# Attention of a hybrid encoder: scores as three products of high and low parts, made in the second projection stage

## Chip, cores and metric

The kernel runs on one core of a Trainium2 chip, as one program with one launch. The metric is device microseconds (us) of one execution. Engines are named as in the profile: PE is TensorE (matmuls), PEld its weight loads, DVE is VectorE, ACT is ScalarE, POOL is GpSimd, SP is SyncE, which here issues most DMAs. An L with a number is a line of the kernel before.

## What is computed

A two-layer encoder over 2048 prompt tokens and 32 sampled tokens, model width 1024. Layer 0 is a gated DeltaNet. From its output h come shared keys and values, and layer 1 is a sliding-window attention over them. The part that the change touches, cut from the reference:

```python
k, v = shared_kv(h, w_kv, pos)               # 4 key heads of 64, partial rotary on k
proj = h @ w_in
q = rope_partial(proj[..., :1024].reshape(b, l, 16, 64), pos) * 64 ** -0.5
z = proj[..., 1024:]
# queries of chunk n (64 tokens) see the keys of chunks n-2, n-1, n
s = jnp.einsum('bnqkgd,bnskd->bnkgqs', qb, kb, preferred_element_type=jnp.float32)
p = sink_softmax(s, sinks)                    # one learned sink logit per head
o = jnp.einsum('bnkgqs,bnskd->bnqkgd', p, vb)
out = (o * jax.nn.silu(z)) @ w_out            # then residual and layer norm
```

## The kernel before

All large products are written as three products of float32r tiles: an operand x is kept as hi = float32r(x) and lo = float32r(x - hi), and hi*hi + hi*lo + lo*hi is accumulated (`project`, L79 to L81). Small products, the scores among them, use plain float32 operands, for which the program has two MATMUL instructions per product.

The work goes through stages: the first projection, the delta rule with layer 0's output beside it, the second projection (its value products start at 1324 us of the span, its last matmul before the hand-written order ends at 1719 us) and attention (first score at 1728.3 us).

**Second projection (class `P2`).** The tokens lie in five blocks of TB = 416 columns. `rotated` makes two key slabs and eight query slabs of 128 rows (i = 0 to 9), each for five blocks b: 24 matmuls into one PSUM bank, of which there are eight here; then `rope` (ACT copies the bank to tile ra at L1343, DVE shuffles it at L1344, POOL multiplies by the sine at L1345, DVE multiplies and adds at L1346 and L1347), and one DMA on SP stores ra to the DRAM scratch bk or bq (L1409, L1412). Tiles ra and rs come from pool `wk` with three buffers, so the bank of block k can be copied only when the store of block k-3 has landed. Beside it, `keep_out_weights` splits the output weights (tiles wo_parts) on ACT and POOL and stores them to the scratch wob. `gate` makes the gate slabs: ACT writes zs and za (L1428, L1429) into the same two tags of pool `wk`, DVE multiplies, and SP stores za to the scratch bz (L1431). The order in this stage comes from the scheduler of the framework.

**Attention (class `Attention`).** The order is written out by hand for all five engines (`manual_schedule`), each of which runs its instructions in that order. Chunks are taken as 14 to 31, then 0 to 13. Before: the keys are loaded in three stretches into one tile kT that stays (`load_keys`, L1491: chunks 12 to 17 first, 18 to 31 next, 0 to 11 last); `start(n)` loads the queries of chunks n and n+1, two DMAs of 256 KB (L1676); `gate(n)` loads their gates (L1681). `scores(n, p)` makes for each of two p four products of 64 rows by 128 by up to 192 columns (L1698), the two halves of which lie on rows 0 to 63 and 64 to 127 of the array. Then softmax (DVE L1518, ACT L1523, POOL L1537), transposes (L1713), copies to tile pt (ACT L1719, DVE L1720), products with the values (`values`, L1731) and, once for two chunks, the output projection (L1146 to L1148) and the layer norm.

At the start of attention eight last blocks of gate slabs 4 to 7 are still to be made; the function `gates` in `program` makes them piece by piece between the first chunks, and among them issues the loads of two weight slabs (L48), of keys and values for the later chunks and of the first output weights (`load_early`, L1468: EARLY = 3 of 8 pieces, 1024 KB each). When the pools of the second projection are closed, `opened` loads the remaining pieces (`load_late`, L1484), and the last keys. The output projection of the first two chunks needs all eight pieces.

Of the kernel before, what the change touches and what calls it, by code (L numbers as in the profile page):

```python
# [22 lines left out]
NP = 2048  # L23
NS = 32
# [1267 lines left out]
class P2:  # L1292
# [100 lines left out]
    def rotated(self):  # L1393
# [6 lines left out]
        for i in range(10):  # L1400
            w = split_weights(nc, self.wp, I["w_k"][i] if i < 2 else I["b_w_in"][i - 2], nc.gpsimd)
            for b in range(NB):
# [4 lines left out]
                if i >= 2:  # L1407
                    a = self.rope(ps[:, :TB], b, 0.125)
                    nc.sync.dma_start(T["bq"][i - 2, :, b * TB:(b + 1) * TB], a[:])  # L1409
                    continue  # L1410
                a = self.rope(ps[:, :TB], b, 1.0)
                nc.sync.dma_start(T["bk"][i, :, b * TB:(b + 1) * TB], a[:])  # L1412
                if b == NB - 1:
                    nc.scalar.dma_start(O["k_last"][i, :, :], a[:, TB - 160:TB])
                    nc.scalar.dma_start(O["s_kT"][i, :, 96:128], a[:, TB - NS:TB])
# [18 lines left out]
class Attention:  # L1434


    EARLY = 3

    def __init__(self, tc, left, I, O, T, G):
# [10 lines left out]
        self.kT = one.tile([128, 2, NP], F32, tag="kT", name="kT")  # L1450

# [37 lines left out]

    def load_keys(self, a, z):  # L1490
        self.nc.sync.dma_start(self.kT[:, :, a * 64:z * 64],  # L1491
                               self.T["bk"][:, :, a * 64:z * 64].rearrange("a p t -> p a t"))
# [119 lines left out]
    def sampled_keys(self):  # L1612
        nc, I, T, one, two = self.nc, self.I, self.T, self.one, self.two
        ks = one.tile([128, 2, 160], F32, tag="ks", name="ks")
        nc.sync.dma_start(ks[:, :, 0:128], I["cache_kT"].rearrange("a p t -> p a t"))
        nc.sync.dma_start(ks[:, :, 128:160], T["bk"][:, :, NP:NT].rearrange("a p t -> p a t"))
        vc = one.tile([128, 256], F32, tag="vc", name="vc")
        nc.sync.dma_start(vc[:], I["cache_v"])
        vn = one.tile([32, 256], F32, tag="vn", name="vn")
        nc.sync.dma_start(vn[:], T["bv"][NP:NT, :])  # L1620
        qs = two.tile([128, 8, NS], F32, tag="qs", name="qs")
        zs = two.tile([128, 8, 128], F32, tag="zs", name="zs")
        nc.sync.dma_start(qs[:], T["bq"][:, :, NP:NT].rearrange("h p t -> p h t"))
# [47 lines left out]
    def start(self, n):  # L1671

        qs = self.two.tile([128, 2, 8, 64], F32, tag="qs", name="qs")
        for i in range(2):
            tk = (n + i) * 64
            self.nc.sync.dma_start(qs[:, i], self.T["bq"][:, :, tk:tk + 64].rearrange("h p t -> p h t"))  # L1676
        self.data[n], self.data[n + 1] = [qs, None], [qs, None]
# [10 lines left out]
    def scores(self, n, p):  # L1688

        nc = self.nc  # L1690
        qs = self.data[n][0]
        kc0, nj = self.keys(n)
        nk = nj * 64
# [537 lines left out]
```

## Time and profile before

| what | value |
|---|---|
| median of 3 runs | 2122.08 us (2119.59 to 2124.72) |
| the profiled execution | 2119.22 us, of which its span 2117.1 us |
| granted TensorE clock in it | 0.996 |
| PE busy | 2078.8 us, 98% of the span |
| POOL, ACT, DVE busy | 39%, 43%, 62% |
| DMA | 307.26 MB, 145 GB/s on the mean |

The profile is one execution. A busy PE is one on which some matmul is under way, since matmuls are pipelined: two rows that start 0.19 us apart may each last 0.35 us. The time between two starts is therefore the pace, the length of a row is not. The view by stretches gives the busy time of each engine between two times, the granted clock, the mean busy share of the 16 DMA engines, and GB/s. The chain of work that ended last follows each instruction back to what released it.

### The profile page before, as it was taken

What the parts mean: (1) busy time and instruction counts of PE and PEld (TensorE: products, weight loads), DVE (VectorE), ACT (ScalarE), POOL (GpSimd) and SP (SyncE); (2) the same over time, 40 slices, a digit from 0 to 9 for tenths busy, and PEclk for the clock granted to TensorE, in tenths of its full rate; (3) what the DMA queues carried; (4) which work ended last, traced back from release to release, by engine and by line L of the source; (5) the groups of instructions that cost most, each with busy time, mean ns of one, the idle gap of its engine ahead of it and who ended that gap; (6) DMA issues with size and microseconds to landing.
All of it is one profiled execution on the core that took longest, in us unless ns stands there. A gap on an engine that the chain in (4) does not pass through costs nothing.

```text
span 2117.1 us, 37205 instructions
## 1 busy us (share of the span) xinstructions
PE 2078.8 (98%) x14062; PEld 1912.6 (90%) x14062; DVE 1306.6 (62%) x2449; ACT 901.1 (43%) x2263; POOL 834.6 (39%) x1179
## 2 busy tenths in 40 slices
PE   8999999999999999999999999999999998999998
PEld 6999999999999999999888888999999996777775
DVE  4676666666557688889978885225543223566665
ACT  4444444445622377677752212322111233455552
POOL 1422222222122187878830302136443103566765
PEclk9999999999999999999999999999999998999999
DMA  5222332346664545556846764455222257534321
GB/s 206 67 65 82 111 111 92 96 128 207 197 197 153 178 157 180 163 171 210 278 159 204 240 194 131 135 196 202 82 72 70 75 143 259 137 100 120 100 72 65
DMA packets 263636, 307.26 MB, mean 145 GB/s; under 512 B 71409, under 2 KB 194609, under 8 KB 263185
## 3 DMA queue, kind: packets, MB, share of 16 engines
q1 hardware_dynamic: 252208, 281.40, 42.7%
q10 hardware_dynamic: 11248, 23.48, 3.4%
q8 instruction: 111, 1.82, 0.4%
q14 instruction: 69, 0.56, 0.1%
HBM read 188.58 MB, written 116.60 MB: 144 GB/s over the span
## 4 chain that ended last, share of the span: by engine, by line
PE 91%; POOL 3%; DMA 2%; DVE 2%; ACT 1%; issue 1%; SPq 1%; ACTq 0%; POOLq 0%; DVEq 0%
PE ps L79 17%; PE ps L81 17%; PE ps L80 17%; PE ot L1146 3%; PE po L1146 3%; PE po L1148 3%; PE po L1147 3%; PE ot L1148 3%; PE ot L1147 3%; PE S L1698 2%; PE ot L1731 2%; PE tr L1713 2%; POOL tm L729 1%; POOL Tt L731 1%; PE g L695 1%; PE gq L831 1%
## 5 line engine op out<-in xcount | busy, mean ns | idle before, releaser
L79 PE MATMUL ps<-act_hi,w_hi 128*128 128x416 f32 x1936 | 683.3, 354 | 1.4 <-ACT act_hi L70 1.4
L81 PE MATMUL ps<-act_hi,w_lo 128*128 128x416 f32 x1936 | 681.3, 352 | 0.9 <-POOL w_lo L56 0.9
L80 PE MATMUL ps<-act_lo,w_hi 128*128 128x416 f32 x1936 | 678.2, 350 | 0.4 <-DVE act_lo L71 0.4
L79 PEld LDWEIGHTS ps<-act_hi,w_hi 128*128 128x128 f32 x1936 | 364.1, 188 | 6.6 <-ACT act_hi L70 2.1
L80 PEld LDWEIGHTS ps<-act_lo,w_hi 128*128 128x128 f32 x1936 | 363.8, 188 | 4.8 <-DVE act_lo L71 0.8
L81 PEld LDWEIGHTS ps<-act_hi,w_lo 128*128 128x128 f32 x1936 | 363.4, 188 | 4.7 <-POOL w_lo L56 1.3
L56 POOL TENSOR_TENSOR w_lo<-w_raw,w_hi 128x1024 fp32r<-128x1024 f32 x44 | 117.1, 2661 | 470.3 <-ACT w_hi L55 443.1
L209 DVE SCALAR_TENSOR_TENSOR y<-R,convw,y 128x2083 f32<-128x2083 f32 x72 | 182.7, 2538 | 62.8 <-ACT y L206 46.9
L1537 POOL TENSOR_TENSOR P<-e,sm 128x384 f32<-128x384 f32 (+2 forms) x128 | 101.2, 812 | 181.7 <-DVE sm L1527 175.7
L729 POOL TENSOR_TENSOR tm<-L,Tt 128x60 f32<-128x60 f32 (+19 forms) x365 | 133.2, 365 | 78.8 <-issue 39.9
L731 POOL TENSOR_TENSOR Tt<-Tt,tm 128x60 f32<-128x60 f32 (+19 forms) x365 | 140.8, 386 | 28.6
L1523 ACT ACTIVATE e<-S,nm 128x193 f32<-128x193 f32 (+2 forms) x260 | 104.8, 416 | 95.9 <-DVE nm L1518 58.2
L1146 PE MATMUL ot<-wo,g_hi 128*128 128x512 f32 x256 | 104.6, 409 | 6.1 <-DMA wo<-s_wob 6.1
L305 ACT COPY R<-ps 128x416 f32<-128x416 f32 (+1 forms) x144 | 60.3, 442 | 108.3 <-PE ps L81 95.7
L1146 PE MATMUL po<-wo_hi,g_hi 128*128 128x512 f32 x256 | 103.3, 404 | 0.2 <-ACT g_hi L1188 0.2
L1345 POOL TENSOR_TENSOR rs<-rs,sin 128x416 f32<-128x416 f32 x50 | 70.7, 1414 | 80.3 <-DVE rs L1344 73.5
L1148 PE MATMUL ot<-wo,g_lo 128*128 128x512 f32 x256 | 101.2, 395 | 0.0
L1147 PE MATMUL ot<-wo,g_hi 128*128 128x512 f32 x256 | 101.1, 395 | 0.0
L1148 PE MATMUL po<-wo_hi,g_lo 128*128 128x512 f32 x256 | 100.2, 392 | 0.5 <-DVE g_lo L1189 0.5
L1430 DVE SCALAR_TENSOR_TENSOR za<-zs,za 128x416 f32<-128x416 f32 x40 | 31.7, 796 | 111.3 <-ACT za L1429 111.1
L1147 PE MATMUL po<-wo_lo,g_hi 128*128 128x512 f32 x256 | 99.9, 390 | 0.0
L55 ACT CAST w_hi<-w_raw 128x1024 fp32r<-128x1024 f32 x46 | 48.3, 1051 | 93.5 <-PE ps L80 74.4
(299 smaller groups left out, 3917.9 us busy)
## 6 DMA issues: line engine op xcount, KB each, us to landing
w_raw<-in_w_in SPq DMA_DIRECT2D x40, 512.0 KB
w_raw<-in_b_w_in SPq DMA_DIRECT2D x18, 512.0 KB
k<-s_k SPq DMA_DIRECT2D x17, 512.0 KB
E<-s_E SPq DMA_DIRECT2D x17, 512.0 KB
s_bz<-za SPq DMA_DIRECT2D x40, 208.0 KB
s_bq<-ra SPq DMA_DIRECT2D x40, 208.0 KB
s_q<-y SPq DMA_DIRECT2D x8, 1024.0 KB
s_wo<-wo_parts SPq DMA_DIRECT2D x16, 512.0 KB
```

Source lines behind the costliest of these rows:

```text
L56: sub.tensor_tensor(out=lo[:], in0=raw[:], in1=hi[:], op=ALU.subtract)
L79: nc.tensor.matmul(ps, hi[:, k, :], xh[:, k, :], start=(k == 0), stop=False)
L80: nc.tensor.matmul(ps, hi[:, k, :], xl[:, k, :], start=False, stop=False)
L81: nc.tensor.matmul(ps, lo[:, k, :], xh[:, k, :], start=False, stop=(k == KC - 1))
L209: nc.vector.scalar_tensor_tensor(out=y[:], in0=R[:, j:j + W], scalar=self.convw[:, i, j:j + 1], in1=y[:], op0=ALU.mult, op1=ALU.add)
L729: P.tensor_tensor(out=tm[:n, i0 - k:, :w], in0=L[:n, i0:, j:j + 1].to_broadcast(sh), in1=Tt[:n, j:j + 1, :w].to_broadcast(sh), op=ALU.mult)
L731: P.tensor_tensor(out=Tt[:n, i0:, :w], in0=Tt[:n, i0:, :w], in1=tm[:n, i0 - k:, :w], op=ALU.subtract)
L1146: nc.tensor.matmul(ps[:n], ghi[:, k, :n], hi, start=a, stop=False)
L1147: nc.tensor.matmul(ps[:n], ghi[:, k, :n], lo, start=False, stop=False)
L1148: nc.tensor.matmul(ps[:n], glo[:, k, :n], hi, start=False, stop=z)
L1523: self.nc.scalar.activation(x.e[:, h, u, :x.n], x.S[:, h, u, :], AF.Exp, bias=x.nm[:, h, u:u + 1], scale=1.0, accum_out=x.sm[:, h, u:u + 1])
L1537: self.nc.gpsimd.tensor_tensor(out=x.P[:, u, :nj * 128].rearrange("r (j h k) -> r j h k", h=2, k=64), in0=x.e[:, :, u, :n].rearrange("r h ...
```

## The change

Queries and keys are split into hi and lo right after the rotary step, and both parts go to new DRAM scratch tensors. Of the old scratch only the 32 sampled columns remain. In attention the keys no longer stay: `start(n)` loads, for two chunks, a stretch of up to 256 keys in both parts (tile kw, two DMAs of 256 KB) and the queries in both parts (four DMAs of 256 KB). A score is hi*hi + lo*hi + hi*lo in float32r, one MATMUL instruction each. EARLY goes from 3 to 2, and the tiles of the sampled step's keys and values take a slot of kw.

```diff
@@ P2.rotated
-                if i >= 2:
-                    a = self.rope(ps[:, :TB], b, 0.125)
-                    nc.sync.dma_start(T["bq"][i - 2, :, b * TB:(b + 1) * TB], a[:])
-                    continue
-                a = self.rope(ps[:, :TB], b, 1.0)
-                nc.sync.dma_start(T["bk"][i, :, b * TB:(b + 1) * TB], a[:])
+                a = self.rope(ps[:, :TB], b, 0.125 if i >= 2 else 1.0)
+                name, j = ("q", i - 2) if i >= 2 else ("k", i)
                 if b == NB - 1:
...
+                self.keep_parts(T["bparts_" + name][:, j, :, b * TB:(b + 1) * TB], a)
+
+    def keep_parts(self, dst, a):
+        nc = self.nc
+        hi = self.wk.tile([128, TB], F32R, tag="rh", name="rh")
+        lo = a[:].bitcast(F32R)
+        nc.scalar.copy(hi[:], a[:])
+        nc.gpsimd.tensor_tensor(out=lo, in0=a[:], in1=hi[:], op=ALU.subtract)
+        nc.sync.dma_start(dst[0], hi[:].bitcast(F32))
+        nc.sync.dma_start(dst[1], a[:])
@@ Attention
-    EARLY = 3
+    EARLY = 2
...
-        self.kT = one.tile([128, 2, NP], F32, tag="kT", name="kT")
...
-    def load_keys(self, a, z):
...
@@ Attention.start
-        qs = self.two.tile([128, 2, 8, 64], F32, tag="qs", name="qs")
+        k0, k1 = max(0, n - 2) * 64, (n + 2) * 64
+        kw = self.two.tile([128, 2, 2, 256], F32R, tag="kw", name="kw")
+        qs = self.two.tile([128, 2, 2, 8, 64], F32R, tag="qs", name="qs")
+        for a in range(2):
+            self.nc.sync.dma_start(kw[:, a, :, :k1 - k0].bitcast(F32),
+                                   self.T["bparts_k"][a, :, :, k0:k1].rearrange("c p t -> p c t"))
...
@@ Attention.scores
         for u in range(2):
-            for half in range(2):
-                hs = slice(half * 64, half * 64 + 64)
-                nc.tensor.matmul(S[:, half, u, :nk], qs[hs, n % 2, p * 4 + 2 * u:p * 4 + 2 * u + 2, :],
-                                 self.kT[hs, p, kc0 * 64:kc0 * 64 + nk], start=True, stop=True)
+            for i, (a, b) in enumerate(((0, 0), (1, 0), (0, 1))):
+                for half in range(2):
+                    hs = slice(half * 64, half * 64 + 64)
+                    nc.tensor.matmul(S[:, half, u, :nk], qs[hs, n % 2, a, p * 4 + 2 * u:p * 4 + 2 * u + 2, :],
+                                     kw[hs, b, p, k0:k0 + nk], start=(i == 0), stop=(i == 2))
```

On SP at the start of attention, from the last load of the sinks to the first output weights, the program before has these rows (kT are keys, qs queries, vd values, zs and s_bz gates loaded and stored, w_raw a weight slab, wo output weights):

```order
L1491 DMA kT<-s_bk 128x2x384
L1676 DMA qs<-s_bq 128x8x64 x2
L48 DMA w_raw<-in_b_w_in 128x1024
L1497 DMA vd<-s_bv 64x6x128 x2
L1676 DMA qs<-s_bq 128x8x64 x2
L1681 DMA zs<-s_bz 128x8x128 x2
L1431 DMA s_bz<-za 128x416 x2
L48 DMA w_raw<-in_b_w_in 128x1024
L1491 DMA kT<-s_bk 128x2x896
L1497 DMA vd<-s_bv 64x14x128 x2
L1468 DMA wo<-s_wob 128x2x1024 x3
```

and the changed one, at the same place, these (kw are the keys of two chunks in both parts; line numbers are those of the changed kernel):

```order
L1679 DMA kw<-s_bparts_k 128x2x256 x2
L1684 DMA qs<-s_bparts_q 128x8x64 x4
L48 DMA w_raw<-in_b_w_in 128x1024
L1499 DMA vd<-s_bv 64x6x128 x2
L1679 DMA kw<-s_bparts_k 128x2x256 x2
L1684 DMA qs<-s_bparts_q 128x8x64 x4
L1690 DMA zs<-s_bz 128x8x128 x2
L1439 DMA s_bz<-za 128x416 x2
L48 DMA w_raw<-in_b_w_in 128x1024
L1499 DMA vd<-s_bv 64x14x128 x2
L1474 DMA wo<-s_wob 128x2x1024 x2
```

More bytes now stand ahead of the first two stores of za, and fewer between them and the next ones, since a stretch of keys and one piece of output weights are gone from there; `load_late` loads six pieces instead of five.

On ACT, for one query slab in the quiet part of the second projection, the program before has these two rows:

```order
L55 CAST w_hi<-w_raw 128x1024
L1343 ACTIVATE ra<-ps 128x416 x5
```

and the changed one has these:

```order
L55 CAST w_hi<-w_raw 128x1024
L1343 ACTIVATE ra<-ps 128x416 x2
L1420 CAST rh<-ra 128x416 x2
L1343 ACTIVATE ra<-ps 128x416
L1420 CAST rh<-ra 128x416
L1343 ACTIVATE ra<-ps 128x416
L1420 CAST rh<-ra 128x416
L1343 ACTIVATE ra<-ps 128x416
L1420 CAST rh<-ra 128x416
```

The cast of a block now stands ahead of the copy of the next bank, so ACT takes a bank only when DVE has finished the block before.

More of the change, by code (lines that the diff above doesn't have):

```diff
@@ L2183 @@
     "hT": (8, 128, NT),
-    "bq": (8, 128, NT),
+    "bq": (8, 128, NS),
+    "bparts_q": (2, 8, 128, NT),
+    "bparts_k": (2, 2, 128, NT),
     "bz": (8, 128, NT),
-    "bk": (2, 128, NT),
+    "bk": (2, 128, NS),
     "bv": (NT, 256),
```

35 lines of the change are left out of this document (17 added, 18 removed).

## Prediction

> **What bounds the kernel now.** I read the page's first and fourth parts, then PE's waits, then the view by stretches.
>
> ```profile
> span 2117.1 us, 37205 instructions
> PE 2078.8 (98%) x14062; PEld 1912.6 (90%) x14062; DVE 1306.6 (62%) x2449; ACT 901.1 (43%) x2263; POOL 834.6 (39%) x1179
> ...
> PE 91%; POOL 3%; DMA 2%; DVE 2%; ACT 1%; issue 1%; SPq 1%; ACTq 0%; POOLq 0%; DVEq 0%
> ```
>
> ```profile
> PE ot L1146 <- DMA wo<-s_wob: 6.1, 4, 2.9
> PE ot L1731 <- ACT za L1429: 1.8, 1, 1.8
> ```
>
> ```profile
> 1500.00:1550.00 50.00, 50.00 (x266) 49.60 (x265) 22.24 (x45) 7.60 (x13) 20.43 (x13) 1.00 0.20 69
> 1728.00:1760.00 32.00, 30.19 (x206) 25.71 (x205) 12.66 (x23) 16.72 (x56) 6.61 (x9) 1.00 1.09 296
> 1780.00:1798.00 18.00, 11.64 (x63) 6.99 (x62) 3.94 (x10) 4.71 (x19) 7.18 (x7) 0.82 0.96 366
> 1880.00:1920.00 40.00, 40.00 (x303) 30.77 (x302) 24.82 (x61) 21.13 (x77) 26.72 (x22) 1.00 0.38 103
> ```
>
> PE is the bound nearly everywhere: in the second projection (first stretch) and in quiet attention (last stretch) it is busy 50.00 of 50 and 40.00 of 40 us, and no other engine has more than 27 of 40. So a score costs what PE spends on it, and work on other engines is free while PE has something to do. There are two exceptions, and both lie at the start of attention. From 1728 to 1760 us the DMA engines are full (share 1.09), and from 1780 to 1798 us they are full again (0.96) while PE idles over 6 us. The two waits above belong there: the gate that waits for its buffer, and the output weights. The change touches all three places: the pace of the scores, the side chain of the second projection, and the bytes at the start of attention.
>
> **The scores.** Before, one call (one chunk, one p) is eight records, in four pairs for the two halves of the rows; after, it is twelve, in six pairs.
>
> ```profile
> L1698 PE MATMUL S<-kT,qs 64*128 64x192 f32 x480 | 56.7, 356 | 0.0
> ```
>
> ```profile
> 1811.06 0.92 PE L1698 MATMUL S<-kT,qs 64*128 64x192 f32 x8
> 1811.91 0.86 PE L1731 MATMUL ot<-pt,vd 64*64 64x256 f32 x9
> ```
>
> ```profile
> 1925.06 0.66 PE L1698 MATMUL S<-kT,qs 64*128 64x64 f32 x8
> 1925.65 0.77 PE L1713 MATMUL tr<-ident,P 128*128 128x128 f32 x5
> ```
>
> 480 records of 192 columns are 60 calls; four more calls have 64 or 128. With 192 columns a call holds PE for 1811.91 - 1811.06 = 0.85 us, with 64 columns for 1925.65 - 1925.06 = 0.59 us. A third of the columns does not cost a third of the time, so something else sets a floor. It is the loading of weights:
>
> ```profile
> 14.83 0.19 PEld L81 LDWEIGHTS ps<-act_hi,w_lo 128*128 128x128 f32 x1 [1.31 <-POOL w_lo L56]
> 14.94 0.19 PEld L79 LDWEIGHTS ps<-act_hi,w_hi 128*128 128x128 f32 x1
> ```
>
> ```profile
> 1354.50 0.28 PE L1388 MATMUL ps<-vh,act_lo 128*128 128x256 f32 x1
> 1354.62 0.28 PE L1389 MATMUL ps<-vl,act_hi 128*128 128x256 f32 x1
> ```
>
> The first two rows are float32r weights of 128 columns after an idle moment: the second load starts 0.11 us after the first. Four steps of 0.11 us and 0.15 us at the ends make the 0.59 us above. The other pair shows float32r products of 256 columns 0.12 us apart, which bounds the step from above. No float32r product has under 256 columns in this trace. I take the step of the new products as 0.11 us, set by the weights, with 0.15 to 0.21 us at the ends (0.85 less four steps of 0.16): 6 x 0.11 + 0.15 to 0.21 = 0.81 to 0.87 us. Bounds: -0.04 us per call by the low end, and 6 x 0.12 + 0.21 - 0.85 = +0.08 us by the high one. I take +0.02 us: 60 x 0.02 = 1.2 us. The four short calls go from 0.59 to about 0.84 us: +1.0 us. Together **+2.2 us** (-1.4 to +5.8): three passes in place of four gain nothing, since six loads replace four pairs of passes.
>
> The Trainium skill, "TensorE: Matmul & The Clock Gate", section "LDWEIGHTS (loading the stationary operand)", gives columns / 1.2 in ns, 107 ns for 128, and the 0.11 us agree. Its section "Weight-path perf modes" says that the fast weight load is on for 128 weights of any type but FP32; with it the load would not be the floor, and the section "Back-to-back issue gap" would give an estimated 82.5 ns for 192 columns. The two rows 0.11 us apart speak against it.
>
> **The side chain of the second projection.** Each of 50 blocks gains one cast on ACT, one subtraction on POOL and one more store of 208 KB.
>
> ```profile
> 1496.92 0.52 ACT L1343 ACTIVATE ra<-ps 128x416 f32<-128x416 f32 x1 [4.06 <-DVE ra L1347]
> ```
>
> ```profile
> 1496.93 3.72 SPq L1409 DMA_DIRECT2D s_bq<-ra  x2
> ```
>
> ```profile
> 1400.00:1450.00 50.00, 50.00 (x266) 49.56 (x266) 19.33 (x36) 12.47 (x22) 28.49 (x21) 1.00 0.65 224
> 1450.00:1500.00 50.00, 50.00 (x266) 49.60 (x265) 30.70 (x54) 10.18 (x18) 31.11 (x21) 1.00 0.48 162
> ```
>
> ```profile
> L1093 POOL TENSOR_TENSOR wo_parts<-wo_parts 128x512 fp32r<-128x512 f32 x16 | 21.1, 1322 | 50.1 <-ACT wo_parts L1092 49.2 <-PE ps L81 0.8
> L1092 ACT CAST wo_parts<-wo_parts 128x512 fp32r<-128x512 f32 x16 | 9.9, 621 | 50.4 <-DMA wo_parts<-in_b_w_out 48.0 <-POOL wo_parts L1093 1.5 <-issue 0.9
> ```
>
> PE makes a block in 24 products of 0.19 us, 4.5 us. From the copy of a bank (1496.92) to the end of its store's issue (1500.65) pass 3.7 us. The cast, scaled from 621 ns for 512 columns, is about 0.5 us: a chain of some 4.1 us, under 4.5. The subtraction, 416/512 x 1322 = 1.1 us, lies on POOL beside the next block's copy and shuffle. In the busiest 50 us POOL has 31.11 us; eleven subtractions make it 43. So I cost this part at **0**; what hides it is the eight banks of PSUM and PE's own 4.5 us. If the cover is gone, the price is the excess of the chain over 4.5 us times 50, less the lead: the next weight slab waits behind the casts on ACT and must be ready five blocks (22.7 us) ahead, some 19 us without its own splitting. Below nothing it can't go, since PE has no idle time there.
>
> **The start of attention.** On SP the hand-written order now has six DMAs in each `start`.
>
> ```profile
> 1726.00:1728.00 2.00, 2.00 (x12) 1.99 (x11) 0.04 (x1) 0.00 (x0) 0.00 (x0) 1.00 1.32 263
> 1744.00:1746.00 2.00, 2.00 (x14) 1.94 (x13) 0.63 (x1) 1.47 (x3) 0.00 (x0) 1.00 1.19 189
> 1750.00:1752.00 2.00, 2.00 (x15) 1.98 (x14) 1.35 (x3) 0.95 (x5) 0.00 (x0) 1.00 1.03 422
> ```
>
> ```profile
> 1733.20 2.39 SPq L1431 DMA_DIRECT2D s_bz<-za  x2
> ```
>
> ```profile
> 1740.08 0.51 ACT L1429 ACTIVATE za<-ot 128x416 f32<-128x416 f32 x1
> ...
> 1746.62 0.48 ACT L1719 COPY pt<-tr 128x384 f32<-128x384 f32 x1
> ```
>
> ```profile
> 1745.27 13.19 DMA s_bz<-za
> 1758.48 0.53 ACT za L1429
> ...
> 1783.19 14.09 DMA wo<-s_wob
> 1797.32 0.80 PE ot L1146
> ```
>
> The store at 1745.27 landed 13 us later, behind all that was queued: landing is in order of issue, and each byte ahead counts. Ahead of the first two stores of za (issued at 1733.20) two `start`s bring 1024 KB of keys and 1024 KB of queries more, and 384 KB of kT less: +1664 KB. At 263 GB/s (the stretch that loads queries) that is 6.5 us; by the slowest and fastest stretches 9.0 and 4.0 us. The fourth gate's za (1740.08) needs the first one's buffer; it didn't wait before, so its store had landed by 1740.1, and now lands by 1746.6. Queued behind it on ACT are exponentials, a weight cast and the copies to pt that end at 1747.1, 7.0 us later of which 2.2 us were idle: 4.8 us of work, now done by 1751.4. PE's product with the values, which started at 1747.2, starts 4.2 us later. Then the sixth gate's za (1758.48), for which PE had waited 1.8 us, finds its buffer free or nearly so, because kT (896 KB) and one piece of wo are gone ahead of that store: 4.2 - 1.8 = **+2.4 us** (0 at 4.0 us, 4.9 at 9.0). The first score itself waits for 384 KB more, 1.5 us, which is contained in that.
>
> Next, PE waits for the last output weights (1783.19 to 1797.32). Six pieces instead of five at 366 GB/s, the rate of that stretch, are 1049/366 = **+2.9 us**, bounds 2.5 (422 GB/s) and 4.0 (263). Later the extra megabyte for each two chunks is 4 us of DMA time in about 20 us of PE's, on a share of 0.38, fetched four chunks ahead: 0, hidden by the products of these chunks.
>
> **Sum.** 2.2 + 0 + 2.4 + 2.9 = +7.5 us. The profiled execution took 2119.22 us and would take 2126.7; the median of the runs is 2.86 us above it, so I forecast 2122.1 + 7.5 = **2129.6 us**. The ends of the terms, -1.4 + 0 + 2.5 and 5.8 + 4.9 + 4.0, give 2123.2 to 2136.8 for this case.
>
> **Rivals.**
> *The columns set the pace (not slower).* If loads hide behind products, the step is 192/256 x 0.12 = 0.09 us: 6 x 0.09 + 0.21 = 0.75 us per call, -0.10 x 60 = -6.0, and with the start of attention -0.7: 2121.4; with the loads of the start at the fast ends -3.5: 2118.6. It decides from a step below 0.095 us. For it: the 256-column rows fit both readings. Against it: two float32r loads 0.11 us apart, and the 0.59 us call. With the estimated 82.5 ns of the skill's section "Back-to-back issue gap" a call takes 0.70 us and the run about 2118.
>
> *Short float32r products run at the pace of float32.* Nothing in the trace has under 256 columns. At 0.16 us a step: 6 x 0.16 + 0.21 = 1.17 us, +0.32 x 60 = 19, 2147; at twice that step 2205.
>
> *The side chain becomes the bound.* If POOL's subtraction and its in-order neighbours stretch the chain to 5.1 us: 50 x 0.6 - 19 = +11, 2141. For it: POOL at 43 of 50 us while the output weights are split, and ACT bound to DVE's last add. Against it: 0.4 us of room in the quiet part.
>
> *The loads are hidden.* PE finds no later landing than before because the queue drains faster: only 2.2 + 2.5, or 2126 and less.
>
> **Chances.** Forecast 0.55 (2123 to 2137); columns 0.17 (2116 to 2123); loads hidden 0.07 (2122 to 2126); slow short products 0.07; side chain 0.14 (2133 to 2155). The range that holds 8 in 10 is 2118 to 2142. About 0.2%, 4.2 us, is what a measurement of this kernel can tell from no change, so slower means above 2126.3. Slower: 0.47 of the forecast, 0.01 of the hidden loads, 0.07 and 0.14, together 0.69; faster 0.10, from the columns; the same 0.21.
>
> **What will show it.** The starts of S rows: 0.11 us apart per pair is right, 0.09 the first rival, 0.16 the second. PE's waits: one for the first score of 1 to 2 us, one before the first L1731 of 3 to 4 us behind a za on ACT, none or little at the sixth za, and wo at 8 to 10 us in total. PE busy 50 of 50 up to 1719 us; any wait there for a PSUM bank or w_lo is the third rival. The prediction is wrong if the time from the first score to the end of the wo wait grows by under 3 or over 10 us, or if a 192-column call leaves 0.81 to 0.93 us.

## The result, and the profile after

| | before | after |
|---|---|---|
| median of the 12 runs taken side by side | 2119.73 us | 2127.99 us |
| ratio | | 1.0033 [1.0024, 1.0042] |
| profiled execution, span | 2119.22, 2117.1 us | 2126.95, 2125.2 us |

The changed kernel is 0.33% slower, 7.0 us by the ratio. 2129.6 us, or +7.5 us, had been forecast.

The page of the changed kernel shows the same bound. PE is still busy 98% of a longer span:

```profile
span 2125.2 us, 38120 instructions
PE 2080.8 (98%) x14318; PEld 1921.1 (90%) x14318; DVE 1321.2 (62%) x2449; ACT 923.9 (43%) x2313; POOL 889.7 (42%) x1229
```

To find where the 8.1 us between the two spans lie, I matched the products on PE other than scores, which stand in the same order in both programs, and read off how much later each one starts. Five pairs are enough. From the timeline of before (start, length, engine, line, tiles):

```profile
1334.70 0.46 PE L79 MATMUL ps<-act_hi,w_hi 128*128 128x416 f32 x1 [0.85 <-ACT act_hi L70]
1718.00 0.35 PE L79 MATMUL ps<-act_hi,w_hi 128*128 128x416 f32 x1
1764.28 0.43 PE L79 MATMUL ot<-act_hi,w_hi 128*128 128x416 f32 x1
1801.77 1.09 PE L1731 MATMUL ot<-pt,vd 64*64 64x256 f32 x16
2106.89 0.39 PE L1148 MATMUL ot<-wo,g_lo 128*128 128x512 f32 x1
```

and the same five in the timeline of after:

```profile
1337.57 0.46 PE L79 MATMUL ps<-act_hi,w_hi 128*128 128x416 f32 x1 [0.20 <-ACT act_hi L70]
1720.88 0.35 PE L79 MATMUL ps<-act_hi,w_hi 128*128 128x416 f32 x1
1768.91 0.44 PE L79 MATMUL ot<-act_hi,w_hi 128*128 128x416 f32 x1
1809.74 1.09 PE L1741 MATMUL ot<-pt,vd 64*64 64x256 f32 x16
2114.80 0.39 PE L1148 MATMUL ot<-wo,g_lo 128*128 128x512 f32 x1
```

The lags are 2.87, 2.88, 4.63, 7.97 and 7.91 us. So 2.9 us are there before the first changed instruction; the second projection adds nothing; the start of attention adds 1.8 us, the wait for the output weights 3.3, and the 300 us behind it nothing. The changed stretch costs 5.1 us. The 2.9 us ahead of it are taken up with the first experiments.

PE's waits from 1700 us on, in the changed kernel (the longer ones):

```profile
PE ot L1146 <- DMA wo<-s_wob: 8.9, 6, 2.9
PE tr L1723 <- DVE pt L1730: 2.3, 1, 2.3
PE tr L1723 <- ACT pt L1729: 0.6, 1, 0.6
PE S L1708 <- DMA qs<-s_bparts_q: 0.2, 1, 0.2
```

The wait for a gate (1.8 us before) has gone, a wait of 2.3 us ahead of the transposes has come, and the wait for the output weights has grown from 6.1 to 8.9 us. The chain of waits shows what stands behind the new one (start, length, what):

```profile
1743.48 5.17 DMA s_bz<-za
1748.68 0.53 ACT za L1437
1749.23 0.59 DVE za L1438
1749.91 0.86 DVE nm L1520
1750.85 1.72 ACT e L1525 x8
1752.57 0.38 ACT pt L1729
1753.00 0.90 PE tr L1723 x3
```

The fourth gate waits until the store of the first has landed; the exponentials and the copy to pt are queued behind it. SP's timeline tells why that store is late:

```profile
1734.37 6.86 SPq L1684 DMA_DIRECT2D qs<-s_bparts_q  x3
1741.27 2.12 SPq L1690 DMA_DIRECT2D zs<-s_bz  x2
1743.48 1.42 SPq L1439 DMA_DIRECT2D s_bz<-za  x2
```

It was issued at 1743.48 us, against 1733.20 before; without the 2.9 us by which everything is late, that is 7.4 us later. Three loads of queries held SP for 6.86 us. The delay lies in the issue; once issued, the store lands in 5.2 us, at 1748.65.

PE's clock has a part in this, too. In the views by stretches (columns: from and to, length, PE, PEld, DVE, ACT and POOL busy, granted clock, DMA share, GB/s) the granted clock is about 0.50 for some 3.4 us behind the wait for the gate in the kernel before, and for 6.8 us from the waits ahead of the transposes on in the changed one; this is the first line and the second:

```profile
1760.80:1764.20 3.40, 3.40 (x21) 2.26 (x16) 0.97 (x3) 1.82 (x9) 0.70 (x1) 0.51 1.14 303
1751.00:1757.80 6.80, 5.85 (x42) 3.66 (x42) 3.35 (x6) 4.68 (x16) 2.07 (x3) 0.50 1.12 278
```

PE's waits at the start of attention have grown from 1.8 to 3.1 us (the wait of 0.2 us that both have left out), and the stretch of PE's work that runs at half the clock is longer, too; the two together are of the size of the 1.8 us.

### The profile page after: what moved, and what is told of

Read it like the earlier page. It is cut to its first block, busy times and chain, and to the rows that moved or that the text cites. A ratio compares the mean times of both kernels' runs of the same rounds, so it can differ in the third digit from the quotient of the medians.

```text
span 2125.2 us, 38120 instructions
## 1 busy us (share of the span) xinstructions
PE 2080.8 (98%) x14318; PEld 1921.1 (90%) x14318; DVE 1321.2 (62%) x2449; ACT 923.9 (43%) x2313; POOL 889.7 (42%) x1229
## 4 chain that ended last, share of the span: by engine, by line
PE 91%; DMA 3%; DVE 2%; POOL 1%; ACT 1%; SPq 1%; issue 1%; ACTq 0%; POOLq 0%; DVEq 0%
PE ps L79 17%; PE ps L81 17%; PE ps L80 17%; PE ot L1146 3%; PE po L1146 3%; PE po L1148 3%; PE po L1147 3%; PE ot L1147 3%; PE ot L1148 3%; PE S L1708 2%; PE ot L1741 2%; PE tr L1723 2%; PE g L695 1%; PE gq L831 1%; PE ks L846 1%; PE sp L846 1%
## 5 line engine op out<-in xcount | busy, mean ns | idle before, releaser
L1420 ACT CAST rh<-ra 128x416 fp32r<-128x416 f32 x50 | 27.0, 540 | 139.6 <-issue 91.0
L215 DVE SCALAR_TENSOR_TENSOR y<-th,y 128x2083 f32<-128x2083 f32 x24 | 55.9, 2328 | 36.5 <-ACT th L213 36.5
```

## The experiments

Each kernel was profiled and timed against the kernel before on the same chip. The table gives the lags to the first profile of before for all of them, at the five places above and at a product of the output projection at 1870.09 us. "Start" is the growth from 1718.00 to 1764.28, "weights" that from 1764.28 to 1801.77, "later" the rest.

| kernel | lag at 1334.70 | at 1718.00 | at 1764.28 | at 1801.77 | at 1870.09 | at 2106.89 | start | weights | later | ratio |
|---|---|---|---|---|---|---|---|---|---|---|
| after | 2.87 | 2.87 | 4.64 | 7.98 | 7.85 | 7.92 | 1.77 | 3.34 | -0.06 | 1.0033 [1.0024, 1.0042] |
| before_again | -0.12 | -0.15 | -2.56 | -2.59 | -2.51 | -2.50 | -2.41 | -0.03 | 0.09 | 1.0003 [0.9992, 1.0013] |
| before_three | -0.25 | -0.47 | -0.96 | 0.23 | 0.62 | 1.04 | -0.49 | 1.19 | 0.81 | 1.0015 [1.0005, 1.0026] |
| before_scratch | 1.30 | 1.27 | 1.96 | 1.81 | 1.82 | 1.79 | 0.69 | -0.15 | -0.02 | 1.0000 [0.9989, 1.0010] |
| early3 | -0.33 | -0.36 | 1.99 | 3.10 | 3.81 | 4.40 | 2.35 | 1.11 | 1.30 | 1.0031 [1.0019, 1.0043] |
| early4 | 1.56 | 1.56 | 8.36 | 7.23 | 7.28 | 8.02 | 6.80 | -1.13 | 0.79 | 1.0040 [1.0028, 1.0053] |
| stores_first | 4.94 | 4.91 | 5.23 | 8.68 | 8.55 | 8.63 | 0.32 | 3.45 | -0.05 | 1.0033 [1.0021, 1.0045] |
| long_runs | 0.36 | 0.36 | 1.12 | 4.57 | 4.44 | 4.51 | 0.76 | 3.45 | -0.06 | 1.0033 [1.0021, 1.0046] |
| side_twice | -0.01 | 18.67 | 21.44 | 24.87 | 24.74 | 24.79 | 2.77 | 3.43 | -0.08 | 1.0117 [1.0101, 1.0132] |
| late20 | -0.29 | -0.32 | 3.12 | 6.81 | 10.55 | 10.61 | 3.44 | 3.69 | 3.80 | 1.0061 [1.0049, 1.0074] |
| best4 | 1.39 | 1.36 | -0.01 | -1.16 | 2.71 | 3.46 | -1.37 | -1.15 | 4.62 | 1.0005 [0.9996, 1.0014] |
| best5 | 1.23 | 1.23 | -0.13 | 0.68 | 1.46 | 2.19 | -1.36 | 0.81 | 1.51 | 1.0002 [0.9992, 1.0012] |
| before_spread | -0.94 | -0.97 | -5.44 | -5.97 | -5.45 | -5.45 | -4.47 | -0.53 | 0.52 | 0.9988 [0.9979, 0.9998] |

**The scatter: before_again and before_scratch.**

> The kernel before, unchanged, once more, for the scatter of one execution. In the two profiles so far the changed kernel is 2.9 us late at the first value product of the second projection (1337.57 against 1334.70 us), ahead of everything that the change touches. If that is scatter between executions, this profile puts the same product anywhere from about 1333 to 1339 us, and the profiles after the change scatter over the same range. If something in the change causes it (the place of the scratch tensors, say), this one stays within 0.5 us of 1334.70, and every variant of the changed kernel lies near 1337.6. From that product to the end all profiles of this kernel should agree within 0.5 us. The ratio to the kernel before is 1.000 within 0.001.

The product at 1334.70 us started at 1334.59, which by the letter speaks for a cause in the change; but the variants of the changed kernel don't lie near 1337.6, as that cause would have it. From there on it is less steady than I had expected: the start of attention took 2.4 us less in this execution of an unchanged kernel. Its wait for the gate is 1.0 us instead of 1.8, and the clock stays at 1.00 where the other execution has 0.51:

```profile
1760.80:1764.20 3.40, 3.40 (x25) 3.15 (x22) 1.80 (x4) 2.10 (x10) 0.23 (x1) 1.00 1.11 270
```

Half the clock for 3.4 us is worth some 1.7 us, and 0.8 + 1.7 are about the 2.4. One profile therefore gives the start term no better than to some 2 us.

```diff
-    "bq": (8, 128, NT),
+    "bq": (16, 128, NT),
-    "bk": (2, 128, NT),
+    "bk": (4, 128, NT),
```

> The kernel before with the scratch tensors of queries and keys made twice as large; only the first half is used, nothing else changes. In the three profiles of kernels with the new scratch PE waits 3.2 to 4.8 us for loads of k near 1006 to 1030 us, in the delta rule, which the change doesn't touch; in the three profiles without it 0 to 0.5 us. If the place of the tensors in memory does that, the waits appear here too (2 us or more), and the ratio is 1.000 to 1.001. If not, they stay under 0.6 us and something else in the changed program, or chance, is the cause.

Its waits for k stayed away, so the size of these tensors is not the cause. Over all profiles the lag at 1334.70 us is -0.94 to +1.30 us in the five of the kernel before and its variants (0.00 on the mean) and -0.33 to +4.94 in the nine of the changed kernel and its variants (1.30 on the mean). PE's waits for k in that part are 0 to 0.5 us in the five and 0.4 to 4.8 in the nine (3.2 in the changed kernel). Early3 has 3.3 us of the same wait and yet no lag (-0.33), so the wait doesn't explain the lag by itself.

In the changed kernel's own profile the 2.9 us can be read off, and they are there before any wait for k. The first product waits for its operand for 8.4 us instead of 7.0, which makes a lag of 1.4 us. It stays so up to 740 us and is 3.0 at 744: there the clock is 0.50 for 3.4 us, in which PE has 17 products where it had 29 before (second line, the same work 1.4 us earlier):

```profile
740.60:744.00 3.40, 3.40 (x17) 2.63 (x15) 0.98 (x4) 3.21 (x13) 2.70 (x10) 0.50 0.52 157
739.20:742.60 3.40, 3.40 (x29) 2.95 (x28) 1.32 (x6) 3.21 (x13) 2.69 (x10) 1.00 0.55 157
```

Best4 and best5 gain 1.6 us of lag at the same place with the same clock. The waits for k near 1010 and 1030 us are made up again by 1050 us, where the lag is 2.9. Whether the changed program brings such a stretch and the longer first wait about stays open: the two ranges of lags overlap from -0.33 to 1.30, and chance isn't excluded.

**The scores alone: before_three.**

```diff
-            for half in range(2):
...
-                nc.tensor.matmul(S[:, half, u, :nk], qs[...], self.kT[...], start=True, stop=True)
+            for i in range(3):
+                for half in range(2):
...
+                    nc.tensor.matmul(S[:, half, u, :nk], qs[...], self.kT[...], start=(i == 0), stop=(i == 2))
```

> The kernel before with its loads and stores unchanged, but each score as three float32r products of the same unsplit tiles (so the split is left out and the scores are three times hi*hi). This is the price of the scores alone. If the weight loads set the pace, a call of 192 columns takes 0.85 us (0.11 us per pair, as in the changed kernel), one of 64 columns about 0.79, and the run stays within 0.1% of the kernel before: from the first value product of the second projection to the end it grows by 0 to 0.5 us. By the prediction's own term it would be +2.2 us, 1.0010. If the columns set the pace, 0.75 us a call, -6 us, 0.997. If the loads of the changed kernel, and not its products, were what makes its calls 0.85 us, the call here is shorter than there.

The chain of this kernel has one call with 192 columns and one with 64 (twelve records each, between other rows):

```profile
1811.79 0.84 PE S L1699 x12
...
1925.70 0.79 PE S L1699 x12
```

and that of the changed kernel:

```profile
1811.27 0.84 PE S L1708 x12
...
1932.87 0.79 PE S L1708 x12
```

A call takes the same time in both, so the loads of the changed kernel add nothing to it. From 192 to 64 columns, a third, it falls by 0.05 us of 0.84: columns don't set the pace. The six pairs of a call start 0.11 us apart but for the first two (0, 0.19, 0.30, 0.42, 0.53 and 0.64 us after the first in the call at 1851.73 us of the changed kernel).

That it is the load, and not something that each product costs whatever its weights, can be read from the kernel before. In the delta rule it has float32 products of the form of its short score calls, 64 rows and 64 columns, but with weights of 64 columns in place of 128:

```profile
749.13 0.68 PE L799 MATMUL y2p<-ta,npr 64*64 64x64 f32 x16
749.74 0.66 PE L818 MATMUL vtr<-ident,v 128*128 128x128 f32 x4
```

Sixteen records, eight pairs, take 0.61 us, 0.06 us from pair to pair; the short call takes 0.59 us for four pairs, 0.11 us from pair to pair. Half the columns of weights, about half the step.

From the start of a call to that of the next work the median over 60 calls is 0.851 us before, 0.845 here and 0.846 in the changed kernel. The Trainium skill, "TensorE: Matmul & The Clock Gate", section "LDWEIGHTS (loading the stationary operand)", gives columns / 1.2 in ns, an estimated 107 ns for 128 columns; these calls agree at 192, 128 and 64 columns, and the fast load of its section "Weight-path perf modes" does not show here: a load of these 64x128 float32r weights lasts 189 ns, and the pairs don't start closer.

As a whole this kernel is longer than I had expected, by a ratio of 1.0015, 3.2 us (1.1 to 5.5), where 0 to 0.5 us were said; the prediction's own term, 2.2 us, is in that interval. In its profile the lag of 1.04 us at the end is -0.96 at 1764.28, 1.19 from the wait for the output weights, though their loads are as before, and 0.81 behind it, of which 0.55 arise between 1921 and 1950 us, where the four short calls lie. The wait is taken up below.

**The side chain: side_twice.**

```diff
         nc.scalar.copy(hi[:], a[:])
+        nc.scalar.copy(hi[:], a[:])
         nc.gpsimd.tensor_tensor(out=lo, in0=a[:], in1=hi[:], op=ALU.subtract)
+        nc.gpsimd.tensor_tensor(out=lo, in0=a[:], in1=hi[:], op=ALU.subtract)
```

The second subtraction works on the result of the first, so the low part has hi taken off twice; the amount of work is what was meant.

> The changed kernel with the cast of the high part and the subtraction of the low part each done twice in every block (same values). In the changed kernel PE is busy 50 of 50 us throughout that stage and the chain of a block repeats every 3.9 us at its fastest against PE's 4.5. Twice as much is 0.54 us more on ACT and 1.1 us more on POOL a block. If the chain is serial, as the prediction had it, a block takes 5.0 to 5.4 us, and 50 blocks cost 25 to 45 us less a lead of some 19: +6 to +26 us on the changed kernel. If banks and order leave more room than that, PE stays at 50 of 50 and the time is that of the changed kernel (1.0033).

The second projection takes 18.7 us more, and little behind it changes (start 2.77, weights 3.43). PE's waits in that stage name the slab of weights that is split behind the blocks, and no bank:

```profile
PE ps L81 <- POOL w_lo L56: 9.6, 5, 4.3
PE ps L79 <- ACT w_hi L55: 2.7, 3, 1.9
```

By stretches (columns as before: PE, PEld, DVE, ACT, POOL), first this kernel, then the changed one:

```profile
1500.00:1550.00 50.00, 50.00 (x266) 49.61 (x265) 31.69 (x42) 16.96 (x32) 43.33 (x35) 1.00 0.31 110
1550.00:1600.00 50.00, 45.01 (x228) 43.47 (x227) 30.87 (x42) 16.97 (x33) 41.98 (x33) 0.97 0.32 112
```

```profile
1450.00:1500.00 50.00, 50.00 (x266) 49.58 (x265) 27.15 (x44) 15.21 (x29) 37.48 (x29) 1.00 0.61 207
1550.00:1600.00 50.00, 50.00 (x266) 49.61 (x265) 25.72 (x48) 12.94 (x26) 34.80 (x26) 1.00 0.36 128
```

PE stays at 50.00 until the lead is used up and then loses about 5 us in each of two stretches of 50. The waits above are 12.3 us; most of the rest of the 18.7 is the clock, 0.97 in each of the three 50-us stretches from 1550 us on, which is half the clock for some 3 us each. Nobody is busy all the time (POOL 43 of 50), and the 50 copies of banks take 260 us, 5.3 a block: it is the serial chain of a block that has become longer than PE's 4.5 us. So the stage is near its bound, and the change stayed on the free side of it.

**One piece fewer ahead: early3 and early4.**

```diff
-    EARLY = 2
+    EARLY = 3
-        kw = self.two.tile([128, 2, 2, 256], F32R, tag="kw", name="kw")
+        kw = self.two.tile([128, 2, 2, 256], F32R, tag="kw", name="kw", bufs=2)
```

(and the same for qs; early4 has EARLY = 4, and the high part goes into rs).

> The changed kernel with three early pieces of the output weights again instead of two; the room comes from two buffers instead of three for the tiles of keys and queries. If the last output weights cost what the prediction says (one piece more, 2.9 us), the end of the wait for them comes 2.5 to 2.9 us earlier against the products ahead of it, and the ratio to the kernel before falls from 1.0033 to about 1.002. If the wait is set by something other than the bytes still to come (a late release of the pools, say), nothing changes: 1.0033. If two buffers are too few, the steady part grows: iterations of 10.15 us become longer and the ratio is above 1.0033.

> The changed kernel with four early pieces of the output weights; the room comes from two buffers for keys and queries, and the high part is written into the tile rs of the same block instead of a tile of its own. With three early pieces the wait for the last weights took 1.5 us less than with two. If each piece still to come costs its bytes (about 2.7 us), the wait falls from 8.9 to 3 or 4 us and the ratio to about 1.001. If the queue in front (loads of chunks 18 to 21, still on their way when the pools are released) sets it, each further piece early only lengthens that queue, and the wait stays above 6 us. Writing the high part into rs costs nothing if a store lands within three blocks of 4.5 us; otherwise PE waits before 1719 us.

Three early pieces bring the weights term from 3.34 to 1.11 us (1.8 if read at 1870.09), four to -1.13. About 2.2 us a piece. PE's wait itself falls by 1.5 us a piece, from 8.9 to 7.3 to 5.8 us, where 3 or 4 had been expected with four. The two buffers cost little: from 1870.09 us to the end the lag of early3 grows by 0.6 us, all of it where the four short calls lie. But with four the start grows from 1.77 to 6.80 us, since the early pieces are issued ahead of the third store of za:

```profile
1751.47 15.71 DMA s_bz<-za
1767.19 0.53 ACT za L1437
```

and the sixth gate, which needs that buffer, holds the products up for 1.9 us again, while the 2.1 us ahead of the transposes stay:

```profile
PE ot L1146 <- DMA wo<-s_wob: 5.8, 3, 2.7
PE tr L1723 <- DVE pt L1730: 2.1, 1, 2.1
PE ot L1741 <- ACT za L1437: 1.9, 1, 1.9
```

The sum is what it was, 1.0031 and 1.0040, where about 1.002 and 1.001 had been expected. That each piece costs its bytes came near at the weights (2.2 us where 2.5 to 2.9 were said) and failed for the whole.

Nor is a piece all that the weights cost. With five late pieces, as many as before, early3 keeps 1.1 of the 3.3 us, and before_three, whose loads are those of before, has 1.2. The time from the issue of the last store of za to the product that ends the wait shows both:

| kernel | scores | late pieces | from, to | us |
|---|---|---|---|---|
| before | float32 | 5 | 1780.12, 1797.32 | 17.2 |
| before_scratch | float32 | 5 | 1782.12, 1799.25 | 17.1 |
| before_three | three passes | 5 | 1779.15, 1797.61 | 18.5 |
| early3 | three passes | 5 | 1782.12, 1800.47 | 18.4 |
| early4 | three passes | 4 | 1788.48, 1804.61 | 16.1 |
| after | three passes | 6 | 1784.76, 1805.98 | 21.2 |

So some 1.2 us come with the scores in three passes. In this stretch the view of the DMA queues has one packet of the kind "instruction" on queue q8 in before_three, in the changed kernel and in all its variants, and none in before, before_again, before_scratch and before_spread. The line of before_three (packets, MB, share of the 16 engines):

```profile
q8 instruction: 1, 0.02, 0.3%
```

By its kind it brings the program's own instructions, of which the kernels with three passes have more (14318 products in the changed kernel instead of 14062, each with its load). Each DMA reports its landing in sixteen parts; of those of the last piece in before_three fifteen come by 1796.21 us and one at 1797.57, while before all sixteen come within 0.40 us. So this packet, it seems, now falls into the wait and holds up one part of each piece behind it. No run moves the packet alone; that it is the cause is argued, not shown.

**The first stores: stores_first and long_runs.**

```diff
-        att.start(16)
-        att.gate(14)
-        att.gate(16)
```

(the three calls now stand behind the second store of za.)

> The changed kernel with the loads of chunks 16 and 17 (keys and queries 1536 KB... 1024 KB of queries, 512 KB of keys, and two gates of 512 KB) moved behind the first two stores of za on SP. If the fourth gate waits because of what stands ahead of the first store, that store is issued about 8 us earlier (near 1735 us instead of 1743.5), its buffer is free before the fourth gate wants it, and the wait in front of the transposes (2.3 us) and the slow first products with the values go: the stretch from the first score to the 40th us behind it gets 2 to 5 us shorter, of which some comes back at the fifth to eighth gates, whose stores now stand behind the moved loads. The ratio falls to 1.0015 to 1.003. If instead the engines are full in any case, the same wait moves to the later gates and the ratio stays at 1.0033.

The first two stores are issued at 1735.1 and 1735.7 us in an execution that is 4.9 us late, and the start term is 0.32 us instead of 1.77. So what stands ahead of the first store did make that wait. It comes back in part at the sixth gate (2.3 us of waiting), as expected. The ratio did not move, 1.0033, which is what I had expected for a wait that only moves. 1.5 us are less than its interval of 5 us shows and lie within the scatter of one profile, and a part of them is the clock (0.97 from 1720 to 1780 us, against 0.94 in the changed kernel).

```diff
-                self.nc.sync.dma_start(qs[:, i, a].bitcast(F32),
-                                       self.T["bparts_q"][a, :, :, tk:tk + 64].rearrange("h p t -> p h t"))
+            self.nc.sync.dma_start(qs[:, i].bitcast(F32), self.T["bparts_q"][:, n + i])
...
-    "bparts_q": (2, 8, 128, NT),
+    "bparts_q": (128, 33, 2, 8, 64),
```

> The changed kernel with the scratch of the query parts laid out by chunk, so that a load of one chunk's queries (both parts, all heads) is one transfer of 4 KB runs in each row instead of two of 256-byte runs; the stores of the second projection take the 256-byte runs (two DMAs for each part). In the changed kernel the issue of one 256 KB load of queries holds SP for 1 to 3.4 us at the start of attention. If those short runs, and not the bytes, make the queue slow there, the first store of za is issued 4 to 8 us earlier than at 1743.5, the wait behind the fourth gate goes, and the stretch from the last product of the second projection to the end of the wait for the output weights shrinks by 2 to 5 us; the ratio to the kernel before falls to about 1.001. If the bytes are what counts (the prediction's 1664 KB at 263 GB/s), the start changes by less than 1 us. If the short runs in the stores hurt, it shows before 1719 us as waits for banks, and the ratio rises.

The loads of queries leave SP at once now, as its timeline shows:

```profile
1727.64 1.96 SPq L1690 DMA_DIRECT2D kw<-s_bparts_k  x2
1729.70 0.90 SPq L1693 DMA_DIRECT2D qs<-s_bparts_q  x2
1732.14 3.36 SPq L1698 DMA_DIRECT2D zs<-s_bz  x2
1735.99 5.38 SPq L1450 DMA_DIRECT2D s_bz<-za  x2
```

0.90 us for 1 MB, where three quarters of that took 6.86 us, and the issue of the first store begins at 1735.99 instead of 1743.48. But this issue then holds SP for 4.9 us itself, and the second one follows at 1741.00, where it was 1744.53 in the changed kernel: without the lags of 0.36 and 2.87 us that is 1.0 us earlier. So most of SP's time has moved from the loads to the store. The first score waits 1.7 us for its queries, the start term falls to 0.76 us only, the stretch up to the end of the wait for the weights shrinks by 0.9 us where 2 to 5 were expected, and the ratio stays at 1.0033. The short runs were a small part of it at most, and the bytes the rest. In the second projection the 256-byte stores cost nothing (lag 0.36 at both ends).

**The queue: late20, best4, best5, before_spread.**

```diff
-            if i == 1:
-                self.start(order[6])
-            elif i == 2:
-                self.gate(order[6])
...
+        self.start(20)
+        self.gate(20)
         self.tabs = ln_tables(...)
```

> The changed kernel with the loads of chunks 20 and 21 (keys, queries, gate: 1536 KB) issued right behind the late output weights instead of ahead of the last stores of za. With four early pieces the wait for output weights fell by 3.1 us, but the fifth and sixth gates waited that much longer, so the queue looks full from 1726 us to the end of the wait, and what counts is the number of bytes in that window. If so, 1536 KB less ahead of the weights bring the end of the wait 3 to 5 us earlier (growth over the wait near 0 instead of +3.3 us against the kernel before), chunk 20's scores then wait at most 2 us, and the ratio falls to about 1.002. If the release of the pools sets the start and the six pieces the end, only the backlog at the release counts, and the gain is under 2 us.

My idea that the bytes of the whole window count falls here. The DMA engines were free between 1770 and 1780 us (share 0.07), the backlog was gone when the pools were released, and the wait for the weights is the same 8.8 us. What sets it is the release and the pieces behind it: from the issue of the last store of za to the product are 21.1 us with six pieces here (1783.28 to 1804.39), where the changed kernel with six has 21.2. And the loads moved behind the weights made a new wait:

```profile
PE ot L1743 <- DVE r L1154: 2.2, 1, 2.2
```

The rows of h for the second output projection now stand behind them and land late; 3.8 us are lost after the weights.

Best4 puts together queries in long runs, only what chunks 14 and 15 need ahead of the first two stores, the early pieces (four) and the gate of 16 behind the fourth store, and chunk 20 and values 22 to 31 behind the late weights.

> All of it together on the changed kernel: queries in 4 KB runs, only two chunks' keys and queries ahead of the first two stores of za, gate loads, values 22 to 31 and early weights behind the fourth store, chunks 20 and 21 and values 22 to 31 behind the late weights, four early pieces (two buffers for keys and queries, high part in rs). If bytes ahead of the stores and ahead of the weights are the whole cost of the change, the start term is 0 or below, the wait for the weights falls to about 4 us, and the kernel ends 4 to 8 us below the changed one: at or up to 4 us below the kernel before, ratio 0.998 to 1.000. If the full queue only moves the waits, chunk 16's or chunk 20's scores or values wait instead and the ratio stays at 1.003 or above.

Start -1.37, weights -1.15: both terms of the change are gone and more. But the rows of h pay again, 3.9 us between 1801.77 and 1870.09:

```profile
1770.00:1780.00 10.00, 10.00 (x96) 8.72 (x96) 4.76 (x10) 5.66 (x22) 3.24 (x4) 1.00 0.06 21
```

```profile
1812.62 9.72 DMA r<-s_h
```

Best5 puts those loads back between the first chunks, where the first of these lines shows the engines free.

> The previous combination, but chunks 20 and 21 loaded at their old place (between the first chunks) and values 22 to 31 right behind them, instead of behind the late output weights. There the combination had a DMA share of 0.06 between 1770 and 1780 us, and paid 3.9 us later: the rows of h for the second pair of chunks stood behind those loads in the queue, landed 9.7 us after their issue, and PE waited 2.2 us for the add that needs them. If that queue is the cause, the growth between 1802 and 1870 us is 0.5 us or less, the wait for the weights stays at 5 to 6 us, and the kernel comes out 2 us below the kernel before: ratio 0.998 to 0.9995. If the loads now slow the weights instead, the wait for them is 8 us or more and the ratio stays at 1.0005.

The loss behind the weights shrinks to 0.8 us, but the wait for them is 6.9 us in place of 5.7, as values 22 to 31 are still landing when the pools are released. The kernel equals the kernel before, 1.0002, and is not below it as I had expected. So the order of the loads, with the long runs and four early pieces, is worth about all that the change cost.

Before_spread applies the same order of loads (with three early pieces) to the kernel before.

> The kernel before with the same rearranged loads (chunks 16 and 17 and their gates behind the first stores, early weights behind the fourth store, chunks 20, 21 and values 22 to 31 behind the late weights), three early pieces, queries in 256-byte runs. It separates the order of the loads from the change: if the order helps by itself, the wait for the gate (1.8 us) and part of the wait for the weights (6.1 us) go here too, ratio 0.997 to 0.999. If the kernel before had no excess of bytes there, nothing changes: 1.000.

It is the only one that is faster than both kernels, 0.9988 [0.9979, 0.9998] against before, 2.5 us (0.4 to 4.5). In its profile most of the gain comes from the start (-4.47 us, of which some 2 are within the scatter, and some 1.7 are the clock, 1.00 from 1720 to 1780 us against 0.97): the wait for the gate is gone, the first two stores are issued at 1726.5 and 1729.0 us instead of 1733.2 and 1735.2. The wait for the weights stays:

```profile
PE ot L1146 <- DMA wo<-s_wob: 6.2, 4, 2.9
PE ot L1734 <- DVE r L1154: 0.4, 1, 0.4
```

So the place between the loads, which the change filled further, cost the kernel before as well. With rearranged loads on both sides, best5 against before_spread, the changed kernel is still 0.0014 behind, some 3 us; the order doesn't make the change free.

## Why the prediction was right, point by point

The forecast of +7.5 us met a measured 7.0 (8.3 between the medians). Its mechanisms held, its terms less so, and that the sum came so near is in part luck. From the first score to the end of the wait for the weights pass 74.8 us instead of 69.0: 5.8 us more, between the 3 and 10 that the prediction set as bounds.

- **The scores, taken as +2.2 us: mechanism right, size too high.** The weight loads set the pace, and three passes in place of four gain nothing. But a call of 192 columns takes 0.846 us, 0.005 us less than before where +0.02 was taken: -0.3 us for 60 calls, between the low bound of -0.04 a call and what was taken. The four short calls go from 0.592 and 0.645 to 0.786 and 0.818 us, +0.7 us where +1.0 was taken. Together +0.4 us, and that is what the lag behind the weights shows in place: 7.98 us at 1801.77, 7.74 at 1921, 8.25 at 1950 behind the four short calls, 7.92 at the end. The step lies at 0.11 us as taken; the ends, 0.2 us, are the same as before. What the sum did not have is that the three-pass scores also come with 1.2 us at the wait for the weights (before_three).
- **The side chain, taken as 0: right, and for the reason given.** The lag at 1718.00 is that at 1334.70. The chain was summed a little short (3.7 + 0.5 us are 4.2, not 4.1); at its fastest a block repeats every 3.9 us. Twice the work costs 18.7 us, in the range of 6 to 26 that follows from the serial chain, and at the weight slab that the prediction named as the price.
- **The start of attention, taken as +2.4 us: 1.8 us in this pair of profiles; with the scatter of before (-2.4 to +0.7 in three more) and 2.8 us in side_twice, where attention is the changed kernel's, some 2 to 3.** The store, the fourth gate and the work behind it on ACT are as predicted: the store was to land by 1746.6 us instead of by 1740.1, and landed at 1748.65, 1745.8 without the lag of 2.9. All of that lay in its issue. But the products with the values came not 4.2 but 5.9 us later (lag 8.8 at 1756.68 us, from 2.9), since they and the transposes ahead of them ran at half the clock. Not 1.8 but 4.1 us came back by 1769 us, for before it was the work behind the gate's wait that had run at half the clock. The sum has no term for the clock, and the two errors cancel by luck. The 1 to 2 us of waiting for the first score did not come; it started at 1731.17, the 2.87 us late that everything ahead of it was.
- **The last output weights, taken as +2.9 us: 3.3 us, and 3.4 in the three other kernels with six pieces at their old place.** The wait is 8.9 us where 8 to 10 was said. But the piece, for which the 2.9 were taken, is 2.2 of it; the 1.1 to 1.2 that early3 and before_three have without it are not in the prediction. That the term came out is in part luck.
- **Later loads, taken as 0: right.** The DMA share of quiet attention rose from 0.38 to 0.57, and PE stays at 40.00 of 40:

```profile
1880.00:1920.00 40.00, 40.00 (x334) 31.87 (x335) 24.84 (x64) 21.44 (x76) 26.46 (x23) 1.00 0.57 149
```

The changed stretch thus cost 5.1 us in the profiles and not 7.5, and the sum came out near the median because something ahead of the change, 2.9 us in this profile and 1.3 on the mean of nine, made up for the scores. That part was not foreseen. In this profile it is the longer first wait and a stretch at half the clock; why the changed kernel should have them more often is not shown.

## What to carry to other kernels

Fewer passes are worth nothing where each pass has its own load of weights and the columns are short: count loads and not cycles of columns, and measure one call before splitting operands. A change that adds loads is paid for where a queue is already full, so look for what is issued behind them on the same queue, stores that free buffers above all; giving such stores and loads another order made the kernel before faster by 2.5 us (0.4 to 4.5). Look at the granted clock when two profiles differ: here it was half for 3.4 us or more, mostly behind a wait of PE, which adds to the wait and differed between executions of one kernel. And when a load is moved out of one crowded place, name the small transfer it will then stand in front of.

## What was not expected of the hardware

- Loads with 256-byte runs hold the issuing engine at a full queue: 768 KB of queries took 6.86 us of SP at the start of attention, 1 MB in 4 KB runs 0.90 us; but the next issue, a store, then held it for 4.9 us.
- Of two profiles of one unchanged kernel the start of attention differed by 2.4 us, of which some 1.7 are 3.4 us at half the granted clock in one of them; PE's own stretches repeat within 0.2 us over 380 us of the second projection.
- A wait for a DMA can grow by 1.2 us without a change in its loads (before_three): a packet of the program's own instructions falls into it in all kernels that show this, and in none of the four that don't.
